# A two-layer hybrid encoder in split fp32: background work tied behind weight splits, loads moved ahead, TensorE's order left to the scheduler

## The chip, the cores and the metric

The kernel runs on one core of a Trainium2 chip. The metric is the device time of one execution in microseconds; the kernel before takes 1553.94 us, the median of three runs (1553.2 to 1554.11).

## What is computed

One sequence of 256 tokens of width 1024 passes two layers. Each layer norms the input, projects it to the inputs of three branches and to their gates, runs the branches, merges them, and ends with a SwiGLU FFN:

```python
h = _rmsnorm(x, norm1_g[l])
(rq, rk, rv, rg, c_q, c_kv, k_rope, s5_u, gate_logits) = jnp.split(h @ w_in[l], split_at, axis=-1)
y_ret = _retention_branch(rq, rk, rv, rg, ...)       # 4 heads, both directions
y_mla = _mla_branch(c_q, c_kv, k_rope, ...)          # latent attention, 8 heads, two inner norms
y_s5 = _s5_branch(s5_u, a_re, a_im, log_dt, ...)     # 64 groups of 64 complex states, both directions, then a GLU
proj = jnp.einsum('bsnk,nkd->bsnd', branches, w_branch[l])
x = x + jnp.sum(sigmoid(gate_logits) * proj, axis=2) @ w_out[l]
h2 = _rmsnorm(x, norm2_g[l])
f_gate, f_up = jnp.split(h2 @ ffn_w_gu[l], 2, axis=-1)
x = x + (silu(f_gate) * f_up) @ ffn_w_down[l]
```

Everything is float32, and the output has the shape of the input.

## The kernel before

**Weights.** All projections multiply a weight tile with activations that lie in SBUF with the tokens along the free axis. A weight tile of 128 x 1024 floats is loaded as `raw` (line 674; five buffers), split into a rounded high part `wh` by ScalarE (line 690) and a remainder `wl` by VectorE (line 691), and used in three matmuls per 128 rows (`mm3`, lines 695 to 697). `half_pair` (lines 735 to 737) does the same for the S5 GLU, half a contraction at a time. A few projections (`fm_pair_native`, line 747) use the raw tile with unsplit float32 matmuls and need no normed input. All loads and stores go through one queue, that of SyncE (SP), by `dma` (line 114).

**Two strands of work.** The trunk (`layer`) emits the projections, the retention heads, the latent attention, the merges and the FFN in program order. S5 is a generator (`s5`) that runs in the background: after each weight tile the trunk calls `tick`, which advances the generator by `step` as long as it has credit; a yield of a number is charged to the credit, a yield of "later" ends the tick. So the program order is the trunk's with S5's instructions woven in.

**S5's parts.** `s5_tables` computes constants from the parameters and sends them through DRAM (`pwd`, `bbd`). `s5_wt` makes one of 16 tables of 128 x 1024 from two loaded constants by two VectorE products and two combinations (lines 547, 548, 551, 552). In layer 0 it does so right before the state matmuls (line 473); layer 1's are made during layer 0's FFN, stored to DRAM (`wtd`) and loaded again in layer 1 (lines 463 and 464). Then come the scan over 32 blocks, and for eight pairs the output tables (`s5_out_tables`, which loads the C matrices through `s`), VectorE products (lines 594 to 596), matmuls (lines 612 and 646), a gather through DRAM (lines 662 and 664) and the GLU.

**Chains that cross engines.** A norm's scale is made in `rstd`: sums by TensorE, a small chain, and a spread matmul (line 834) that is put off to the next weight tile's end by `defer` and `flush`. `ret_heads` normalises a head on VectorE and ScalarE and transposes it on TensorE (line 988) in `finish`, one head later. `early_gates` computes some gate tiles ahead of their use, stores them and loads them back; how many stand between the latent norm's chain and its spread matmul is set by `ng0` and `ng1`.

**What sets the order.** Program order is a priority. A scheduler with a model of the chip places the instructions of each engine's queue by priority and by when their inputs are ready in its model. TensorE is the exception: `run` wraps the whole trunk in `manual_schedule` for TensorE, so its instructions stand in program order.

Of the kernel before, what the change touches and what calls it, by code (L numbers as in the profile page):

```python
# [1 line left out]

# [69 lines left out]
class Kern:  # L72
    def __init__(self, ctx, tc, aps, n4=17, n16=2, nraw=5, nw=3, nwl=3, nwy=4, nwt=2, ntm=2, nev=4, nat=3, r0=75, r1=75, r2=20, delay=1, late=0, e0=2, e1=0, force=0, q0=55, q1=60, nat_u=1, gauss=1, unn=1, ya=0, sp=1, yw=40, yy=30, split=2, m0=4, m1=4, fin=1, dfr=1, nu0=3, nu1=1, pin=0, nl=-1, fw=0, fy=1, ng0=0, ng1=2, tt=1, tp=0, nq0=0, nq1=0, sk=1):
        self.sk = sk
        self.nq = nq0, nq1
        self.tt, self.tp = tt, tp > 0
        self.fw, self.fy = fw, fy
        self.pinm, self.nl = pin, nl
        self.pin = pin > 0
        self.later, self.nu = [], (nu0, nu1)  # L80
        self.fin = fin
# [61 lines left out]
    def step(self):  # L143
        try:
            if self.late:
                with self.tc.high_priority(offset=-self.late):
                    c = next(self.bg)
            else:
                c = next(self.bg)
        except StopIteration:  # L150
            self.bg = None
            return
        if c is None:
            self.credit = min(self.credit, 0.0)
            return
        if c == "later":
            return c
        self.credit -= c
# [124 lines left out]
    def s5_tables(self, l):  # L283
# [72 lines left out]
        return dict(ld={}, PWD=PWD, BBD=BBD, BB2D=BB2D, PXD=PXD, A8=A8, A8s=A8s)  # L356

    def s5_out_tables(self, l, tb, qh):


        nc, V, A = self.nc, self.nc.vector, self.nc.scalar
        cn = self.s4().rearrange("p (d t r q) -> p d t r q", d=2, t=4, r=2)
        for d in range(2):
            for r, k in enumerate(("s5_c_re", "s5_c_im")):
                self.dma(cn[:, d, :, r, :],
                                  self.a[k][l, d, qh * 32:qh * 32 + 32].rearrange("(t g) c p -> (g c) t p", t=4))
        BB2 = self.s(2 * 528, "t_bb2", 1).rearrange("p (d x) -> p d x", d=2)
# [33 lines left out]
    def s5(self, l, ctx, gel_out):  # L401
# [52 lines left out]

        lq = None
        for j in range(8):
            wts = []
            for qq in (2 * j, 2 * j + 1):
# [3 lines left out]
                else:  # L462
                    wt = self.s(1152, "wy")[:, 0:1024]
                    self.dma(wt, wtd[qq])
# [11 lines left out]
            lq = self.s(1152, "wy")[:, 0:512]  # L476
# [78 lines left out]
    def s5_out(self, l, tb, du_load, gel_out):  # L555
# [3 lines left out]
        for j in range(8):  # L559
            qh = j // 4  # L560
            if j % 4 == 0:
                if job:
# [5 lines left out]
                BB2, C1, C2, AB = yield from self.s5_out_tables(l, tb, qh)  # L568
# [33 lines left out]
            yield "later"  # L602
            if job:
                self.s5_emit(job)
# [72 lines left out]
    def wsplit(self, view):  # L677
# [8 lines left out]
        self.parts(f(wh), f(wl), view)  # L686
        return f(wh), f(wl)

    def parts(self, hi, lo, src):
        self.nc.scalar.copy(hi, src)  # L690
        self.nc.vector.tensor_tensor(lo, src, hi.bitcast(F32), ALU.subtract)  # L691
# [251 lines left out]
    def ret_heads(self, l, h, q, k, vt):  # L943
# [52 lines left out]
        last = None  # L996
        for hd in range(RH):
# [4 lines left out]
            if last:  # L1002
                finish(*last)
# [3 lines left out]
            last = hd, yn, th  # L1007
            if not self.fin:
                finish(*last)
                last = None  # L1010
        return y, lambda: finish(*last) if last else None

    def mla_down(self, l, h, rest):
# [11 lines left out]
        ps = self.fm_pair(w, OFF_CQ + 256, h.get)  # L1025
        A.copy(cq[:, 512:768], ps[:, 0:S])
# [197 lines left out]
    def layer(self, l, x2, acc, xg, last):  # L1224
# [7 lines left out]
        pre = [native(0)] if self.nu[l] else []  # L1232
        self.flush(True)
# [121 lines left out]
        r = self.rstd(acc, [D])  # L1355
# [42 lines left out]
    def run(self):  # L1398

        with self.tc.manual_schedule(engines={mybir.EngineType.PE}):  # L1400
            self.trunk()

    def trunk(self):
# [30 lines left out]
        self.begin(0)  # L1434
        self.step()
# [85 lines left out]
```

## Time and profile before

| | us |
|---|---|
| median of three runs | 1553.94 (1553.2 to 1554.11) |
| the profiled execution's own time | 1557.51 |
| its span, first to last instruction | 1555.7 |
| busy: TensorE, VectorE, ScalarE | 1331.0, 1066.0, 757.7 |
| mean granted clock of TensorE | 0.935 |

The profile is one execution of the program. Busy time is that in which an engine executes; idle time before an instruction is put down to what released it last. A row of the timeline is a run of like instructions, with the idle time before it and its releaser in brackets. A window's row gives busy time and instruction count of each engine in a stretch, and the mean granted clock of TensorE, 1.00 for 2.4 GHz and 0.50 for 1.2 GHz.

### The profile page before, as it was taken

How to read it: one execution, taken by the hardware profiler on the slowest of the kernel's cores; microseconds unless marked ns; L12 is line 12 of the kernel's file. 1: busy time of each engine (PE TensorE's matmuls, PEld its weight loads, DVE VectorE, ACT ScalarE, POOL GpSimd, SP SyncE). 2: the span in 40 equal slices, each digit the busy share in tenths (PEclk: the TensorE clock that was granted, in tenths of full speed). 3: DMA queues.
4: the chain of work that ended last, by engine and by line, in shares of the span. 5: the costliest groups of instructions: out<-in, count | busy, mean ns of one | idle time of the engine just before them, and what ended most of it. 6: DMA issues, size and time to landing. Idle time of an engine off the chain costs nothing. (4 is left out here: it accounts for less than half of the span.)

```text
span 1555.7 us, 27234 instructions
## 1 busy us (share of the span) xinstructions
PE 1331.0 (86%) x10858; PEld 1254.1 (81%) x10858; DVE 1066.0 (69%) x1904; ACT 757.7 (49%) x1223; POOL 4.4 (0%) x33
## 2 busy tenths in 40 slices
PE   4967768679888999889888798878997989999997
PEld 3856667679788999879887776768996989999997
DVE  6866877778494887767656665686857735767754
ACT  2633344775633554334333454678555434544442
POOL 0000000000000000000000000000000000000000
PEclk9978888889999999999999999978999989999999
DMA  6858753547765775988788896427675656656662
GB/s 191 271 213 237 197 148 119 137 121 190 205 193 178 216 232 187 266 228 215 206 234 239 249 280 207 132 85 191 182 210 162 193 165 191 175 170 184 187 174 87
DMA packets 425043, 297.46 MB, mean 191 GB/s; under 512 B 29954, under 2 KB 387540, under 8 KB 424916
## 3 DMA queue, kind: packets, MB, share of 16 engines
q1 hardware_dynamic: 424916, 295.73, 66.3%
q8 instruction: 85, 1.39, 0.4%
q14 instruction: 42, 0.34, 0.1%
HBM read 265.01 MB, written 30.67 MB: 190 GB/s over the span
## 5 line engine op out<-in xcount | busy, mean ns | idle before, releaser
L695 PE MATMUL pw<-s,wh 128*128 128x256 f32 x2440 | 720.9, 295 | 37.3 <-ACT wh L690 29.9
L697 PE MATMUL pw<-s,wl 128*128 128x256 f32 x2440 | 708.5, 290 | 43.2 <-DVE wl L691 43.1
L696 PE MATMUL pw<-s,wh 128*128 128x256 f32 x2440 | 707.1, 290 | 6.4 <-DVE s L770 4.1
L690 ACT CAST wh<-raw 128x1024 fp32r<-128x1024 f32 (+4 forms) x394 | 380.7, 971 | 510.2 <-PE pw L696 310.5
L691 DVE TENSOR_TENSOR wl<-raw,wh 128x1024 fp32r<-128x1024 f32 (+4 forms) x394 | 442.9, 1127 | 222.9 <-ACT wh L690 216.4
L695 PEld LDWEIGHTS pw<-s,wh 128*128 128x128 f32 x2440 | 482.7, 198 | 49.9 <-ACT wh L690 32.2
L697 PEld LDWEIGHTS pw<-s,wl 128*128 128x128 f32 x2440 | 482.1, 198 | 49.0 <-DVE wl L691 48.8
L696 PEld LDWEIGHTS pw<-s,wh 128*128 128x128 f32 x2440 | 482.7, 198 | 10.9 <-DVE s L770 5.3
L547 DVE TENSOR_TENSOR wy<-s,s 128x1024 f32<-128x1024 f32 x32 | 39.1, 1222 | 68.3 <-DMA s<-bbd 55.6
L735 PE MATMUL pw<-s,wh 128*128 128x256 f32 x256 | 75.5, 295 | 6.2 <-ACT s L766 6.0
L736 PE MATMUL pw<-s,wh 128*128 128x256 f32 x256 | 75.0, 293 | 1.8 <-DVE s L767 1.8
L737 PE MATMUL pw<-s,wl 128*128 128x256 f32 x256 | 74.7, 292 | 0.8 <-DVE wl L691 0.8
L735 PEld LDWEIGHTS pw<-s,wh 128*128 128x128 f32 x256 | 51.2, 200 | 7.4 <-ACT s L766 6.5
L769 ACT ACTIVATE s<-ev 128x512 fp32r<-128x512 f32 x46 | 29.2, 634 | 50.9 <-DVE ev L1367 30.7
L736 PEld LDWEIGHTS pw<-s,wh 128*128 128x128 f32 x256 | 51.3, 201 | 2.3 <-DVE s L767 2.3
L737 PEld LDWEIGHTS pw<-s,wl 128*128 128x128 f32 x256 | 51.2, 200 | 1.0 <-DVE wl L691 1.0
L594 DVE TENSOR_TENSOR wy<-s,s 128x512 f32<-128x512 f32 x64 | 42.9, 687 | 11.9 <-ACT s L393 8.0
L473 PE MATMUL p<-wy,s 128*32 128x256 f32 x256 | 21.2, 438 | 26.2 <-DVE wy L552 15.2
L595 DVE TENSOR_TENSOR tm<-s,s 128x512 f32<-128x512 f32 x64 | 43.1, 685 | 0.2
L596 DVE TENSOR_TENSOR wy<-wy,tm 128x512 f32<-128x512 f32 x64 | 42.9, 685 | 0.0
L747 PE MATMUL pw<-s,raw 128*128 128x256 f32 x128 | 30.2, 395 | 14.5 <-DMA raw<-in_w_in 14.5
L510 ACT COPY s<-s 64x256 f32<-64x256 f32 (+1 forms) x64 | 40.7, 636 | 1.9 <-DVE s L496 1.1
(290 smaller groups left out, 1504.5 us busy)
## 6 DMA issues: line engine op xcount, KB each, us to landing
raw<-in_w_in SPq DMA_DIRECT2D x122, 512.0 KB
raw<-in_ffn_w_gu SPq DMA_DIRECT2D x88, 512.0 KB
raw<-in_w_branch SPq DMA_DIRECT2D x48, 512.0 KB
s<-pwd SPq DMA_DIRECT2D x64, 256.0 KB
s<-bbd SPq DMA_DIRECT2D x64, 256.0 KB
raw<-in_s_w_glu SPq DMA_DIRECT2D x32, 512.0 KB
raw<-in_ffn_w_down SPq DMA_DIRECT2D x32, 512.0 KB
wt<-kd SPq DMA_DIRECT2D x64, 128.0 KB
```

The source lines that it names most:

```text
L510: A.copy(*todo.pop(0))
L594: V.tensor_tensor(y[:, :, js, :], tv(0), cv(C1), ALU.mult)
L595: V.tensor_tensor(t2, tv(1), cv(C2), ALU.mult)
L596: V.tensor_tensor(y[:, :, js, :], y[:, :, js, :], t2, ALU.add)
L690: self.nc.scalar.copy(hi, src)
L691: self.nc.vector.tensor_tensor(lo, src, hi.bitcast(F32), ALU.subtract)
L695: T.matmul(ps, lh, rh, start=first, stop=False)
L696: T.matmul(ps, lh, rl, start=False, stop=False)
L697: T.matmul(ps, ll, rh, start=False, stop=last)
L735: T.matmul(o, wh[:, k, c], xh, start=(half == 0 and m == 0 and k == 0), stop=(k == 3), **f)
L736: T.matmul(o, wh[:, k, c], xl, start=False, stop=(k == 3), **f)
L737: T.matmul(o, wl[:, k, c], xh, start=False, stop=(k == 3), **f)
```

## The change

1. `run` no longer wraps the trunk in `manual_schedule`: TensorE's order comes from the scheduler, as the other engines' does.
2. The weight split returns its two instructions (ScalarE's and VectorE's), and `step` ties every background instruction it emits behind the last of them, each on its own engine (`issue_after`; an order of issue, no semaphore).
3. `s5_tables` ends with the loads for the first two tables and three yields of "later".
4. The C loads (`s5_load_c`) are taken out of `s5_out_tables` and stand ahead of the gather.
5. Layer 1's stored tables are loaded one pair ahead, and `lq` moves to another buffer.
6. One more "later" in the S5 output after pairs 0 and 4.
7. `ret_heads` keeps two heads' `finish` back instead of one; `mla_down` calls `rest` twice.
8. `ng0` goes from 0 to 3 and `ng1` from 2 to 3 (four more tiles stored and loaded).
9. S5's first step stands after the first native projection instead of before the vectors' loads.
10. Norm 2's spread matmul is put off by one more weight tile.

```diff
-    def __init__(..., ng0=0, ng1=2, ...):
+    def __init__(..., ng0=3, ng1=3, ...):
...
     def step(self):
         try:
-            if self.late:
-                with self.tc.high_priority(offset=-self.late):
-                    c = next(self.bg)
-            else:
+            with ExitStack() as st:
+                for i in self.split_at:
+                    st.enter_context(self.tc.issue_after(i.ins))
                 c = next(self.bg)
...
-        return dict(ld={}, PWD=PWD, BBD=BBD, BB2D=BB2D, PXD=PXD, A8=A8, A8s=A8s)
+        tb = dict(ld={}, PWD=PWD, BBD=BBD, BB2D=BB2D, PXD=PXD, A8=A8, A8s=A8s)
+        for q in range(2):
+            self.s5_fetch(tb, q)
+        for _ in range(3):
+            yield "later"
+        return tb
...
+        ahead = reload(0)
         for j in range(8):
-            wts = []
+            wts, ready = [], ahead
+            ahead = reload(j + 1)
...
-                    wt = self.s(1152, "wy")[:, 0:1024]
-                    self.dma(wt, wtd[qq])
+                    wt = ready.pop(0)
...
             if j % 4 == 0:
+                cn = self.s5_load_c(l, qh)
                 if job:
                     for _ in range(3):
                         yield "later"
                     self.s5_emit(job)
                     yield from self.s5_gather(job, du_load, gel_out)
...
             yield "later"
+            if j % 4 == 0:
+                yield "later"
...
-        self.parts(f(wh), f(wl), view)
+        self.split_at = self.parts(f(wh), f(wl), view)
...
-            if last:
-                finish(*last)
+            if len(last) == 2:
+                finish(*last.pop(0))
...
         ps = self.fm_pair(w, OFF_CQ + 256, h.get)
+        rest()
...
         pre = [native(0)] if self.nu[l] else []
+        if l == 0:
+            self.begin(0)
+            self.step()
         self.flush(True)
...
-        r = self.rstd(acc, [D])
+        r = self.rstd(acc, [D], 1)
...
     def run(self):
-        with self.tc.manual_schedule(engines={mybir.EngineType.PE}):
-            self.trunk()
-    def trunk(self):
...
-        self.begin(0)
-        self.step()
```

How the instructions move at three places follows, as they stand in the queues of the built programs (lines of the changed kernel are some 2 to 22 higher).

SP at the start of the program, ahead of it only the loads of the input and the vectors: `raw` are weight tiles, the `s` tiles are S5's parameters. Before:
```order
L114 DMA sgn<-in_sgn 128x2
L114 DMA s_17_137<-in_s_b_re 32x1x1024 x4
L114 DMA s_18_138<-in_s_b_im 32x1x1024 x4
L114 DMA s_19_147<-in_s_a_re 32x1x64 x4
L114 DMA s_19_147<-in_s_a_im 32x1x64 x4
L114 DMA raw_231<-in_w_in 128x8x128
L114 DMA raw_267<-in_w_in 128x8x128
L114 DMA raw_365<-in_w_in 128x8x128
L114 DMA raw_375<-in_w_in 128x8x128
```
Now:
```order
L116 DMA sgn<-in_sgn 128x2
L116 DMA raw_154<-in_w_in 128x8x128
L116 DMA raw_190<-in_w_in 128x8x128
L116 DMA s_35_203<-in_s_b_re 32x1x1024 x4
L116 DMA s_36_204<-in_s_b_im 32x1x1024 x4
L116 DMA nt_ldt_214<-in_s_log_dt 32x1x1 x4
L116 DMA s_37_213<-in_s_a_re 32x1x64 x4
L116 DMA s_37_213<-in_s_a_im 32x1x64 x4
L116 DMA raw_320<-in_w_in 128x8x128
L116 DMA raw_330<-in_w_in 128x8x128
```
Two weight tiles stand ahead of S5's loads, and the step sizes (`nt_ldt`, which before were earlier in the queue) join those.

VectorE in layer 0's FFN; `wl` is a split's remainder, `wy` a table being made for layer 1, and the last number of a name counts tiles in program order. Before:
```order
L691 TENSOR_TENSOR wl_1191_7011<-raw_1189_7008,wh_1190_7010 128x1024
L547 TENSOR_TENSOR wy_1244_7421<-s4_1206_7142,s4_1205_7139 128x1024
L1366 TENSOR_TENSOR ev_1184_6969<-pw_1176_6907,rs256_1064_6199 128x512
L691 TENSOR_TENSOR wl_1195_7042<-raw_1193_7039,wh_1194_7041 128x1024
L1367 TENSOR_TENSOR ev_1184_6969<-ev_1183_6968,ev_1184_6969 128x512
L548 TENSOR_TENSOR wy_1245_7422<-s4_1206_7142,s4_1205_7139 128x1024
L691 TENSOR_TENSOR wl_1198_7072<-raw_1196_7069,wh_1197_7071 128x1024
L770 SCALAR_TENSOR_TENSOR s16_1066_6201<-ev_1184_6969,s16_1066_6201 128x512
L551 TENSOR_TENSOR wy_1244_7421<-wy_1244_7421,wy_1245_7422 128x8x64
```
Now (lines 566 to 571 are 547 to 552 before, 713 is 691):
```order
L713 TENSOR_TENSOR wl_1173_6846<-raw_1171_6843,wh_1172_6845 128x1024
L1388 SCALAR_TENSOR_TENSOR ev_1168_6833<-ev_1168_6833,ev_1169_6834 128x512
L713 TENSOR_TENSOR wl_1176_6876<-raw_1174_6873,wh_1175_6875 128x1024
L566 TENSOR_TENSOR wy_1179_6909<-s4_1141_6630,s4_1140_6627 128x1024
L1389 TENSOR_TENSOR ev_1169_6834<-pw_1161_6772,rs256_1070_6209 128x512
L567 TENSOR_TENSOR wy_1180_6910<-s4_1141_6630,s4_1140_6627 128x1024
L1390 TENSOR_TENSOR ev_1169_6834<-ev_1168_6833,ev_1169_6834 128x512
L570 TENSOR_TENSOR wy_1179_6909<-wy_1179_6909,wy_1180_6910 128x8x64
L571 TENSOR_TENSOR wy_1179_6909<-wy_1179_6909,wy_1180_6910 128x8x64
L713 TENSOR_TENSOR wl_1185_6921<-raw_1183_6918,wh_1184_6920 128x1024
```
Before, the table tile 7421 stands ahead of splits that the program has some 380 tiles earlier; now a table stands behind the split of number 6876 and ahead of 6921, its place in the program.

TensorE near the end of layer 0's S5, where `p5` are S5's output banks and `pw` with lines 735 to 737 is the GLU. Before:
```order
L696 MATMUL pw_888_4868<-s16_538_2795,wh_893_4901 128x256
L697 MATMUL pw_888_4868<-s16_538_2795,wl_894_4902 128x256
L646 MATMUL p5_895_4929<-wy_860_4660,s4_796_4250 32x128 x4
L646 MATMUL p5_895_4929<-wy_860_4660,s4_797_4252 32x128 x4
L646 MATMUL p5_895_4929<-wt_883_4829,s4_795_4248 32x128 x4
L646 MATMUL p5_895_4929<-wy_863_4671,s4_796_4250 32x128 x4
L646 MATMUL p5_895_4929<-wy_863_4671,s4_797_4252 32x128 x4
L646 MATMUL p5_895_4929<-wt_883_4829,s4_795_4248 32x128 x4
L735 MATMUL pw_897_4959<-s4_774_4148,wh_899_4962 128x256
L736 MATMUL pw_897_4959<-s4_775_4149,wh_899_4962 128x256
```
Now (757 to 759 are 735 to 737 before, 668 is 646, 634 is 612):
```order
L719 MATMUL pw_878_4752<-s16_565_2988,wl_884_4786 128x256
L668 MATMUL p5_885_4813<-wy_855_4598,s4_832_4470 32x128 x3
L668 MATMUL p5_885_4813<-wy_855_4598,s4_833_4472 32x128 x4
L668 MATMUL p5_885_4813<-wt_867_4691,s4_831_4468 32x128 x4
L634 MATMUL p5_886_4839<-wy_871_4707,t_bb2_820_4404 32x128 x8
L757 MATMUL pw_895_4884<-s4_818_4400,wh_897_4887 128x256
L758 MATMUL pw_895_4884<-s4_819_4401,wh_897_4887 128x256
L757 MATMUL pw_900_4920<-s4_818_4400,wh_902_4923 128x256
L758 MATMUL pw_900_4920<-s4_819_4401,wh_902_4923 128x256
L668 MATMUL p5_904_4951<-wy_868_4696,s4_832_4470 32x128 x4
L668 MATMUL p5_904_4951<-wy_868_4696,s4_833_4472 32x128 x4
L634 MATMUL p5_905_4977<-wy_890_4865,t_bb2_820_4404 32x128 x8
```
Before, an S5 block and a GLU half follow each other whole. Now the first matmuls of two GLU halves and two S5 output blocks are interleaved, the blocks ahead of their place.

## Rows read from the trace of the kernel before

**Rows 1.** The page: the span, busy time of each engine, and the granted clock in 40 slices.
```profile
span 1555.7 us, 27234 instructions
...
PE 1331.0 (86%) x10858; PEld 1254.1 (81%) x10858; DVE 1066.0 (69%) x1904; ACT 757.7 (49%) x1223; POOL 4.4 (0%) x33
...
PEclk9978888889999999999999999978999989999999
```

**Rows 2.** The waits of TensorE: us in total, times, longest us.
```profile
PE pw L697 <- DVE wl L691: 43.1, 22, 5.1
PE pw L695 <- ACT wh L690: 29.9, 9, 6.1
PE pa L834 <- ACT ev L827: 15.3, 5, 6.2
PE p L473 <- DVE wy L552: 15.2, 2, 10.3
...
PE pa L988 <- ACT at L981: 14.4, 2, 7.4
PE p L473 <- DMA wy<-wtd: 10.9, 6, 3.6
```

**Rows 3.** Windows: us, busy PE PEld DVE ACT POOL (instructions), granted clock, DMA share, GB/s.
```profile
85.00:107.00 22.00, 6.79 (x39) 4.92 (x38) 13.74 (x16) 1.63 (x2) 0.00 (x0) 0.61 0.55 196
160.00:245.00 85.00, 59.53 (x407) 52.58 (x409) 65.22 (x162) 34.33 (x61) 0.48 (x3) 0.82 0.60 164
345.00:490.00 145.00, 130.97 (x1454) 121.28 (x1454) 102.94 (x147) 75.65 (x141) 1.40 (x10) 0.96 0.70 194
603.00:905.00 302.00, 258.85 (x1957) 250.80 (x1957) 206.74 (x266) 116.91 (x150) 0.00 (x0) 0.94 0.84 235
```

**Rows 4.** Timeline of SP and TensorE, 8 to 38 us: start, us, engine line operation, idle before.
```profile
9.45 2.88 SPq L114 DMA_DIRECT2D s<-in_s_b_re  x4
...
21.01 6.22 SPq L114 DMA_DIRECT2D raw<-in_w_in  x5
...
25.28 5.25 PE L747 MATMUL pw<-s,raw 128*128 128x256 f32 x16 [14.49 <-DMA raw<-in_w_in]
...
37.14 1.03 PE L747 MATMUL pw<-s,raw 128*128 128x256 f32 x4
```

**Rows 5.** Timeline of VectorE and TensorE, 90 to 103 us.
```profile
91.75 1.22 DVE L547 TENSOR_TENSOR wy<-s,s 128x1024 f32<-128x1024 f32 x1 [4.22 <-DMA s<-bbd]
...
95.58 1.08 PE L473 MATMUL p<-wy,s 128*32 128x256 f32 x8 [10.27 <-DVE wy L552]
```

**Rows 6.** Windows of three stretches at half clock.
```profile
89.90:107.00 17.10, 6.48 (x36) 4.82 (x37) 12.08 (x14) 0.59 (x1) 0.00 (x0) 0.50 0.58 213
...
199.10:209.30 10.20, 6.13 (x18) 4.74 (x19) 6.30 (x18) 2.28 (x4) 0.00 (x0) 0.50 0.45 122
...
946.60:950.00 3.40, 3.13 (x21) 1.47 (x17) 0.11 (x1) 0.59 (x1) 0.00 (x0) 0.50 1.11 352
```

**Rows 7.** Timeline of TensorE, the spread matmuls of both layers' latent norms.
```profile
237.79 2.08 PE L834 MATMUL pa<-ev,ones 128*128 128x512 f32 x2 [4.69 <-ACT ev L827]
...
1023.43 2.08 PE L834 MATMUL pa<-ev,ones 128*128 128x512 f32 x2 [6.22 <-ACT ev L827]
```

**Rows 8.** The waits of TensorE and VectorE, 603 to 905 us.
```profile
PE pw L697 <- DVE wl L691: 29.8, 13, 4.7
PE pw L695 <- ACT wh L690: 7.6, 3, 4.8
...
DVE wy L547 <- DMA s<-bbd: 47.6, 11, 8.0
```

**Rows 9.** Timeline of VectorE, 673 to 676 us.
```profile
673.86 1.22 DVE L547 TENSOR_TENSOR wy<-s,s 128x1024 f32<-128x1024 f32 x1 [8.04 <-DMA s<-bbd]
```

**Rows 10.** The page's costliest groups: busy, mean ns, idle before and its releaser.
```profile
L691 DVE TENSOR_TENSOR wl<-raw,wh 128x1024 fp32r<-128x1024 f32 (+4 forms) x394 | 442.9, 1127 | 222.9 <-ACT wh L690 216.4
...
L594 DVE TENSOR_TENSOR wy<-s,s 128x512 f32<-128x512 f32 x64 | 42.9, 687 | 11.9 <-ACT s L393 8.0
```

More of the change, by code (lines that the diff above doesn't have):

```diff
@@ L1 @@
 import math
+from contextlib import ExitStack
 import numpy as np
@@ L72, with __init__ @@
 class Kern:
-    def __init__(self, ctx, tc, aps, n4=17, n16=2, nraw=5, nw=3, nwl=3, nwy=4, nwt=2, ntm=2, nev=4, nat=3, r0=75, r1=75, r2=20, delay=1, late=0, e0=2, e1=0, force=0, q0=55, q1=60, nat_u=1, gauss=1, unn=1, ya=0, sp=1, yw=40, yy=30, split=2, m0=4, m1=4, fin=1, dfr=1, nu0=3, nu1=1, pin=0, nl=-1, fw=0, fy=1, ng0=0, ng1=2, tt=1, tp=0, nq0=0, nq1=0, sk=1):
+    def __init__(self, ctx, tc, aps, n4=17, n16=2, nraw=5, nw=3, nwl=3, nwy=4, nwt=2, ntm=2, nev=4, nat=3, r0=75, r1=75, r2=20, delay=1, late=0, e0=2, e1=0, force=0, q0=55, q1=60, nat_u=1, gauss=1, unn=1, ya=0, sp=1, yw=40, yy=30, split=2, m0=4, m1=4, fin=1, dfr=1, nu0=3, nu1=1, pin=0, nl=-1, fw=0, fy=1, ng0=3, ng1=3, tt=1, tp=0, nq0=0, nq1=0, sk=1):
         self.sk = sk
@@ L80, in __init__ @@
         self.later, self.nu = [], (nu0, nu1)
+        self.split_at = ()
         self.fin = fin
@@ L366, in s5_out_tables @@
                                   self.a[k][l, d, qh * 32:qh * 32 + 32].rearrange("(t g) c p -> (g c) t p", t=4))
+        return cn
+    def s5_out_tables(self, l, tb, qh, cn):
+        nc, V, A = self.nc, self.nc.vector, self.nc.scalar
         BB2 = self.s(2 * 528, "t_bb2", 1).rearrange("p (d x) -> p d x", d=2)
@@ L453, in turn, with reload @@
                 A.copy(o(slice(64, 128), -1), ptv[64:128, r])
+        def reload(j):
+            out = []
+            for qq in (2 * j, 2 * j + 1) if wtd and j < 8 else ():
+                wt = self.s(1152, "wy")[:, 0:1024]
+                self.dma(wt, wtd[qq])
+                out.append(wt)
+            return out
         lq = None
+        ahead = reload(0)
         for j in range(8):
-            wts = []
+            wts, ready = [], ahead
+            ahead = reload(j + 1)
             for qq in (2 * j, 2 * j + 1):
@@ L475, in s5 @@
                              wts[i][:, g4], start=True, stop=True, tile_position=(0, g4 * 32))
-            lq = self.s(1152, "wy")[:, 0:512]
+            lq = self.s(1024, "wt")[:, 0:512]
             A.copy(lq.rearrange("p (q r d x) -> p q d r x", q=2, d=2, r=2),
@@ L567, in s5_out @@
                     job = None
-                BB2, C1, C2, AB = yield from self.s5_out_tables(l, tb, qh)
+                BB2, C1, C2, AB = yield from self.s5_out_tables(l, tb, qh, cn)
                 yq = self.s4().rearrange("p (t q c) -> p t q c", t=8, q=8)
@@ L685, in wsplit @@
             f = lambda t: t.rearrange("p (a b c) -> p a b c", a=shp[0], b=shp[1])
-        self.parts(f(wh), f(wl), view)
+        self.split_at = self.parts(f(wh), f(wl), view)
         return f(wh), f(wl)
     def parts(self, hi, lo, src):
-        self.nc.scalar.copy(hi, src)
-        self.nc.vector.tensor_tensor(lo, src, hi.bitcast(F32), ALU.subtract)
+        return (self.nc.scalar.copy(hi, src),
+                self.nc.vector.tensor_tensor(lo, src, hi.bitcast(F32), ALU.subtract))
     def mm3(self, ps, lh, ll, rh, rl, first, last):
@@ L995, in ret_heads @@
         dec = score(0)
-        last = None
+        last = []
         for hd in range(RH):
@@ L1006, in ret_heads @@
                 dec = score(hd + 1)
[L1007 to L1011, printed above, removed]
+            last.append((hd, yn, th))
+        return y, lambda: finish(*last.pop(0)) if last else None
     def mla_down(self, l, h, rest):
```

3 lines of the change are left out of this document (1 added, 2 removed).

## The prediction, made blind

> **What bounds the kernel now.** I read the summary page first: busy time and clock [rows 1]. TensorE works for 1331.0 of 1555.7 us, VectorE for 1066.0, ScalarE for 757.7. The program is bound by TensorE with holes in it: some 225 us of the span it is not at work, and in the clock line some slices after the start show less than 9 tenths. The list of what TensorE waited for [rows 2] splits the holes: weight splits come late (43.1 us for the VectorE half, line 691, and 29.9 us for the ScalarE half, line 690), the S5 state matmuls of line 473 wait for tables (15.2 us in two waits) and for reloaded tables (10.9 us in six), the retention transposes of line 988 wait 14.4 us, the spread matmul of a norm, line 834, 15.3 us. The windows [rows 3] say how much each stage could give: 85 to 107 us is the S5 states' start, 160 to 245 the end of retention and the latent attention's first norm, 345 to 490 the merges over the end of S5, 603 to 905 layer 0's FFN, where layer 1's S5 tables are built beside it. TensorE is the longest engine in all but the first two; in those VectorE has more to do.
>
> **The change part by part.** The sum stands against the profiled execution, 1557.51 us; the median of the runs is 3.6 us below it, and that is taken off at the end.
>
> *The start.* Before, 16 S5 loads stand ahead of the weights on SP [rows 4]: they are issued from 9.45, the first weight tile at 21.01, and TensorE idles 14.49 us until 25.28. Now two tiles stand in front. The first pair can start 21.01 − 9.45 = 11.6 us earlier, at 13.7. The tiles after it queue behind 20 S5 loads: five groups of four at 2.88 us end near 24.6, and with the 4.3 us that the first tile took from issue to use (25.28 − 21.01) the third one feeds TensorE at 28.9; the row of before has 37.14. That is −8 us; ends 0 (the norm chain holds it) and −11.6. The S5 loads are two issues later, some 1.4 us at 0.72 each; the first S5 table is not needed before 91 us, and has its own term next.
>
> *First state matmuls.* At 95.58 TensorE idles 10.27 us, the longer of the two waits (15.2 us together) [rows 2], for a table that VectorE starts at 91.75 after 4.22 us of waiting for a load [rows 5]. Now the two loads go out when the S5 constants end, and three more weight tiles pass before the table is asked for. Behind the first wait TensorE runs 17.1 us at a granted clock of 0.50, 1.2 GHz, and does 6.48 us of work in it [rows 6]; at full clock half of that, 3.2 us, comes back. Ends 0 and −18.4 (15.2 + 3.2). I take −16: the loads are early enough for all of the waits, but some of the VectorE work remains.
>
> *Retention finish and gate tiles, 160 to 245.* The deferred finish puts a further head of projections between the normalised values and the transposes that waited 14.4 us in two equal waits [rows 2]. Three gate tiles instead of none lie between the norm's chain and its spread matmul, which waited 4.69 us [rows 7]. One of the half-clock stretches of this stage holds 6.13 us of work [rows 6], another 3.1 us back. That makes 22, but VectorE is busy for 65.22 of the 85 us [rows 3], so no more than 19.8 can go. Ends 0 and −19.8; I take −13, two thirds, since VectorE would have to run without a gap for all of it. The eight added transfers are four tiles stored and loaded again, some 5.8 us of SP's time at 0.72; the DMA engines are 0.60 busy in that stage, and nobody waits for SP there. If they cost something it is 5.8 us, inside the ends.
>
> *Layer 0's FFN, 603 to 905.* Idle is 302 − 258.85 = 43.2 us; of it 29.8 are waits for the VectorE split and 7.6 for ScalarE's. VectorE itself stands 47.6 us in front of table products whose constants have not landed [rows 8], once for 8.04 us [rows 9], with the splits behind it. The ties put each table behind the splits traced before it. Ends 0 and −43. I take −24, four fifths of the 29.8, as the loads themselves still come through the same queue; the 7.6 stay. By the Trainium skill, page "DMA: Bandwidth & Descriptors", section "Where 436 GB/s comes from", the memory gives a core some 358 GB/s; at the 235 GB/s of this stage (302 us, 71 MB) that would be 198 us, transfers would bound nothing, and the sum would be up to 19 us lower, near 1463. The row has the DMA engines 0.84 busy at that rate, so the transfers are nearer to a bound than the page has it, and I go by the row.
>
> *Reload one pair ahead (layer 1).* Six waits, 10.9 us, and 3.13 us of work in one half-clock stretch [rows 6], which gives 1.6 back. Ends 0 and −12.5; I take −11, since a tile that is asked for a pair earlier has several weight tiles of time.
>
> *Norms.* The layer 1 norm's spread matmul waited 6.22 us [rows 7] and gets three tiles where it had two; norm 2's is put off by one tile, and has part of the 15.3 − 4.69 − 6.22 = 4.4 us that are left of that wait. Ends 0 and −10.6; I take −7.
>
> *Later S5 output.* Longer holds, the C loads moved up and the extra yield squeeze the four pairs of the second half into fewer places of TensorE's order: 316, counted in the order, instead of 460. VectorE has 48 products there (line 594 is one of three such lines, 64 of each over two layers of eight pairs, so 12 a pair) at 0.687 us, 33 us, and some nine splits at 1.13 us [rows 10], 43 together. TensorE's 316 places are 28 us at the stage's mean of 130.97 / 1454 = 0.09 us. So +15 us; ends 0 (with weight matmuls between) and +25, when the gating products come on top. The C loads come earlier and cost nothing: their wait is short already.
>
> *Splits elsewhere.* Of the 73.0 us of waits for splits, 37.4 are in the FFN; 35.6 are left in S5's and attention's stages. Ends 0 and −36. The ties help where a background product stood in front, but ScalarE and VectorE are as full as TensorE there. I take −8.
>
> *TensorE's order.* Instruction counts are the same on TensorE. Against program order 111 pieces have moved, about two dozen of them S5 blocks 60 to 240 places early. Nothing in the trace prices them; the ends are 0 and 118 us (the second rival). In the main case I take 0, as an early block sits where a split would have been awaited.
>
> Sum: −8 − 16 − 13 − 24 − 11 − 7 + 15 − 8 = −72. 1557.5 − 72 = 1485.5, less 3.6: **1482 us**.
>
> **The rivals.** *First, other waits take the place:* only the start, the first states and the reload pay in full (−35), half of the gate, FFN, norm and split terms pays (−26), and the later S5 output costs its 25. Sum −36: 1518 us. For it: VectorE is at 69% over the span and the DMA engines at 0.84 in the FFN, so a hole that is closed may open one behind it. Against it: TensorE is the longest engine in the two longest of the stages shown.
>
> *Second, slower:* TensorE executes blocks where the order puts them, and a block that stands early holds every weight matmul behind it. If two dozen early blocks each wait for the time of the shorter of the two table waits, 4.93 us (15.2 − 10.27), that is 118 us: −72 + 118 = +46, 1600 us. It decides when the mean stall is over 72 / 24 = 3 us. For it: at 95.58 TensorE was idle 10.27 us with such a block at its head, and the ties now make the block's VectorE work later while its place on TensorE is earlier. Against it: the scheduler knows the ties when it places the blocks. The Trainium skill, page "TensorE: Matmul & The Clock Gate", section "Step-by-step: what each phase is for", says that matmuls stay in program order and only weight loads are pulled ahead; by that rule, with which the 10.27 us wait agrees, no hardware reordering would mend such an order.
>
> *Third, all is covered:* all terms at their lower ends and no new stall: −11.6 − 18.4 − 19.8 − 43 − 12.5 − 10.6 − 36 = −152, 1402 us. For it: TensorE's own work is 1331 us and shrinks further at full clock. Against it: the transfer share in the FFN.
>
> *Fourth, nothing happens:* the moves trade one wait for another of its size, 1554 us.
>
> **How the numbers follow.** The forecast has a chance of 0.50, the first rival 0.20, the second 0.15, the third 0.10, the fourth 0.05. The forecast's own range is 1450 to 1515, from its terms' choices going a third of the way to either end. Eight in ten reaches from 1425, short of the third rival, to 1556, above the fourth, and leaves out the second. A measurement of this kernel tells some 0.2% (3 us) from no change. Faster 0.80, same 0.05, slower 0.15.
>
> **What would show it.** Right: TensorE's first projection starts near 14 us; the waits of line 473's successor shrink from 26 us to under 5; the two 7 us waits ahead of the retention transposes are gone; in the FFN stage VectorE no longer waits for table constants and TensorE's idle time is near 20 us; a wait for VectorE products appears late in S5's output of layer 0. Wrong: S5 blocks at TensorE's head with long idle in front of them (second rival), FFN idle as before at the same DMA share (first rival), or half-clock stretches in new places that eat the gain.

## The result, and the profile after

The changed kernel takes 1515.11 us (median of four runs, 1507.58 to 1520.05); the kernel before, run beside it, 1553.57. The ratio is 0.9747, 95% interval 0.9716 to 0.9777: 38.5 us less (1553.57 − 1515.11), where 72 were forecast. The profiled execution took 1519.22 us, against 1557.51.

The page of the changed kernel, against [rows 1]:
```profile
span 1517.1 us, 27238 instructions
...
PE 1336.3 (88%) x10858; PEld 1245.4 (82%) x10858; DVE 1057.9 (70%) x1904; ACT 755.7 (50%) x1223; POOL 4.3 (0%) x33
...
PEclk9988798989988799999998999979999999999999
```
TensorE does the same number of instructions in about the same busy time; what shrank is its idle time, from 224.7 us (1555.7 − 1331.0) to 180.8 (1517.1 − 1336.3).

The waits of TensorE after (us in total, times, longest us; line 717 is 695 before, 719 is 697, 668 is 646, 492 is 473, 448 transposes S5's input and was 438, and 988 is the retention matmul that was 966, while the transposes of line 988 are now line 1010 and wait 0.6 us):
```profile
PE pw L717 <- ACT wh L712: 35.4, 16, 7.1
PE p L668 <- DMA wt<-kd: 21.2, 21, 5.4
PE pw L719 <- DVE wl L713: 17.9, 25, 1.9
PE p L492 <- DVE wy L571: 11.7, 6, 3.8
...
PE p L448 <- ACT s L442: 9.7, 1, 9.7
...
PE pa L988 <- DVE at L981: 6.3, 2, 6.1
```
Against [rows 2], the wait for VectorE's split fell from 43.1 to 17.9 us and the two 7 us waits of the retention transposes are gone. The wait for ScalarE's split did not shrink (29.9 to 35.4), the wait for `kd`, a reload in S5's output, is now the second longest (21.2 us after 8.1), S5's state matmuls still wait 11.7 us, and the transposes of its input wait 9.7 us, once.

To see where the time went I cut both executions by the count of TensorE's instructions: the first 4000, the next 1500, the next 3500 and the rest. The cuts lie early in layer 0's FFN, at the start of layer 1, and behind layer 1's S5 and GLU, short of its FFN; near them the order of the two kernels differs by little. The windows (columns as in [rows 3]) of the kernel before:
```profile
0.00:616.90 616.90, 495.05 (x4001) 455.85 (x4002) 447.04 (x918) 315.60 (x550) 3.56 (x27) 0.92 0.65 189
616.90:846.90 230.00, 197.98 (x1502) 193.11 (x1501) 158.10 (x212) 82.65 (x104) 0.00 (x0) 0.93 0.86 232
846.90:1321.60 474.70, 415.61 (x3503) 384.18 (x3502) 310.45 (x572) 257.49 (x447) 0.80 (x6) 0.93 0.64 188
```
and of the changed kernel:
```profile
0.00:621.70 621.70, 514.53 (x4000) 461.34 (x4001) 440.94 (x918) 311.91 (x548) 3.49 (x27) 0.90 0.64 190
621.70:831.00 209.30, 189.25 (x1503) 184.61 (x1502) 155.79 (x207) 81.18 (x99) 0.00 (x0) 0.96 0.86 255
831.00:1286.90 455.90, 410.96 (x3503) 378.51 (x3502) 311.00 (x577) 261.02 (x453) 0.80 (x6) 0.94 0.65 197
```
TensorE's counts agree within one, an instruction on the edge of a window. Layer 0 up to its FFN takes 4.8 us longer (621.70 after 616.90), the FFN stage 20.7 less, layer 1 to its FFN 18.8 less, and the rest 3.9 less (1517.1 − 1286.9 against 1555.7 − 1321.6). The forecast had −30 for the first of these stages (start −8, first states −16, retention −13, S5 output +15, splits −8), −24 for the second, −18 for the third: two of three came out, and the first missed by 35 us.

The rows split each stage into busy and idle time of TensorE. In the first stage the idle time fell as well, from 121.85 us to 107.17; what rose is the busy time of the same matmuls, from 495.05 us to 514.53, at a mean granted clock of 0.90 after 0.92. The lower clock would make some 11 us of that (an estimate: 495.05 × 0.92 / 0.90 is 506.05); the rest is open. In the FFN stage 12.0 of the 20.7 us are idle time, and 8.7 are busy time at a clock of 0.96 after 0.93.

### The profile page after: what moved, and what is told of

The parts are those of the page before. It is cut to its first block, busy times and chain, and to the rows that moved or that the text cites. A ratio compares the mean times of both kernels' runs of the same rounds, so it can differ in the third digit from the quotient of the medians.

```text
span 1517.1 us, 27238 instructions
## 1 busy us (share of the span) xinstructions
PE 1336.3 (88%) x10858; PEld 1245.4 (82%) x10858; DVE 1057.9 (70%) x1904; ACT 755.7 (50%) x1223; POOL 4.3 (0%) x33
## 5 line engine op out<-in xcount | busy, mean ns | idle before, releaser
L717 PE MATMUL pw<-s,wh 128*128 128x256 f32 x2440 | 708.9, 291 | 45.0 <-ACT wh L712 35.4
L719 PE MATMUL pw<-s,wl 128*128 128x256 f32 x2440 | 700.8, 288 | 17.9 <-DVE wl L713 17.9
L718 PE MATMUL pw<-s,wh 128*128 128x256 f32 x2440 | 698.2, 287 | 0.2 <-DVE s L789 0.2
L717 PEld LDWEIGHTS pw<-s,wh 128*128 128x128 f32 x2440 | 473.6, 194 | 57.1 <-ACT wh L712 41.4
L719 PEld LDWEIGHTS pw<-s,wl 128*128 128x128 f32 x2440 | 472.5, 194 | 27.4 <-DVE wl L713 25.5
L718 PEld LDWEIGHTS pw<-s,wh 128*128 128x128 f32 x2440 | 474.2, 194 | 3.1 <-issue 1.5
L757 PE MATMUL pw<-s,wh 128*128 128x256 f32 x256 | 74.4, 294 | 5.4 <-ACT s L788 3.5
L759 PE MATMUL pw<-s,wl 128*128 128x256 f32 x256 | 73.8, 290 | 3.5 <-DVE wl L713 3.5
L758 PE MATMUL pw<-s,wh 128*128 128x256 f32 x256 | 73.8, 289 | 0.2 <-DVE s L789 0.2
L757 PEld LDWEIGHTS pw<-s,wh 128*128 128x128 f32 x256 | 50.4, 199 | 7.1 <-ACT s L788 3.9
L759 PEld LDWEIGHTS pw<-s,wl 128*128 128x128 f32 x256 | 50.3, 197 | 4.6 <-DVE wl L713 4.4
L758 PEld LDWEIGHTS pw<-s,wh 128*128 128x128 f32 x256 | 50.4, 197 | 0.5 <-DVE s L789 0.5
L769 PE MATMUL pw<-s,raw 128*128 128x256 f32 x128 | 36.6, 453 | 12.7 <-DVE s L1412 7.6
L668 PE MATMUL p<-wt,s 128*32 128x128 f32 x256 | 28.4, 308 | 21.2 <-DMA wt<-kd 21.2
L769 PEld LDWEIGHTS pw<-s,raw 128*128 128x128 f32 x128 | 29.1, 232 | 18.8 <-DVE s L1412 8.0
```

Of the source, the lines that this page charges most:

```text
L668: T.matmul(po[g4 * 32:g4 * 32 + 32, i * 128:i * 128 + 128], lhsT, rhs, start=(k == 0), stop=(k == 2), tile_position=(0, g4 * 32))
L717: T.matmul(ps, lh, rh, start=first, stop=False)
L718: T.matmul(ps, lh, rl, start=False, stop=False)
L719: T.matmul(ps, ll, rh, start=False, stop=last)
L757: T.matmul(o, wh[:, k, c], xh, start=(half == 0 and m == 0 and k == 0), stop=(k == 3), **f)
L758: T.matmul(o, wh[:, k, c], xl, start=False, stop=(k == 3), **f)
```

## The experiments

The change has three parts that can be had apart: the **ties** (point 2 of the change), the **freed order** of TensorE (point 1) and the **moves** (points 3 to 10). My prediction put everything on ties and moves and nothing on the freed order. The rival theory: the freed order is the gain. Six kernels give all the combinations that were missing.

**Ties and moves, TensorE in program order.** The changed kernel, with

```diff
     def run(self):
+        with self.tc.manual_schedule(engines={mybir.EngineType.PE}):
+            self.trunk()
+    def trunk(self):
```

> The changed kernel with TensorE back in program order (ties and moves only). Theory: the freed order is worth nothing by itself, and the loss of some 28 us near the end of layer 0's S5 comes of the ties and moves: 1510 to 1525 us, with that loss still there. Rival, the freed order holds TensorE at S5 blocks that stand early: 1485 to 1500 us, and the loss goes. Second rival, the freed order is what gains: 1530 to 1555 us.

Measured: 1557.57 us, ratio to before 1.0021 (1.0000 to 1.0043). Above the second rival's range by a little, and far from my theory's: without the freed order the whole of the gain is gone.

**Moves and freed order, no ties.** The changed kernel, with

```diff
-        self.split_at = self.parts(f(wh), f(wl), view)
+        self.parts(f(wh), f(wl), view)
```

> The changed kernel without the ties (moves and freed order). Theory: the ties carry the 26 us won in layer 0's FFN; without them the FFN idles as before, and the S5 output loss of layer 0 shrinks: 1520 to 1540 us. Rival, the ties cost more at the S5 output than they win in the FFN: under 1510 us. Rival, the freed order needs the ties: over 1550 us.

Measured: 1507.2 us, 0.9689 (0.9661 to 0.9717). The ties do not carry the gain: without them the kernel is some 0.6% faster than with them (the intervals just touch).

**Freed order alone.** The kernel before, with

```diff
-        with self.tc.manual_schedule(engines={mybir.EngineType.PE}):
-            self.trunk()
+        self.trunk()
```

> The kernel before with TensorE's order freed and nothing else. Theory (order worth about nothing): 1545 to 1565 us. Rival, order gains: under 1540 us. Rival, S5 blocks stand early and hold TensorE: over 1570 us.

Measured: 1514.07 us, 0.9731 (0.9701 to 0.9762). One line gives as much as the whole change. My theory of an order worth nothing falls here.

**Ties alone.** The kernel before, with the edits to `step`, `wsplit` and `parts` that the change shows, and `split_at = ()` at the start.

> The kernel before with the ties alone, TensorE in program order. Theory: the FFN gains its 24 us and the table waits are not touched, some of it is given back where S5's output is held behind splits: 1525 to 1545 us. Rival, the ties alone do nothing without the early loads: 1550 to 1556 us. Rival, they hold the S5 work on the path: over 1560 us.

Measured: 1542.69 us, 0.9917 (0.9888 to 0.9945): the ties are worth some 0.8%, as my theory had it.

**Moves alone:** the two edits of the first and second experiment together.

> The moves alone: no ties, TensorE in program order. The four runs so far give freed order alone 1514, with the moves 1507, with moves and ties 1515, ties and moves without it 1558, ties alone 1543. If the parts add up, moves alone are 1545 (1552 less the 7 they win beside the freed order). Rival, the moves need the freed order, as their late pieces hold a TensorE in program order: 1555 to 1575 us.

Measured: 1569.48 us, 1.0096 (1.0069 to 1.0123). The moves by themselves are slower. Beside the freed order their median is the better one (0.9689 against 0.9731), but the intervals overlap. The parts do not add up.

**Ties and freed order:** the edits of the third and fourth together.

> Ties and freed order without the moves. If the parts add up: 1514 less the 10 that the ties win alone, 1504 us. Rival, the ties take from the freed order the blocks that it fills holes with, as they do beside the moves (plus 8): 1518 to 1525 us.

Measured: 1506.05 us, 0.9696 (0.9671 to 0.9720). By the medians the ties add 8.0 us to the freed order (1514.07 − 1506.05), near the sum's 10; the intervals of the two ratios overlap.

The stages, cut as above, show which part does what. Each is one profiled execution, in us; executions of one kernel differ by up to some 12 us (the changed kernel's by 1520.05 − 1507.58), so a difference of a few us between two rows says nothing:

| kernel | first 4000 | FFN, 1500 | layer 1, 3500 | rest |
|---|---|---|---|---|
| before | 616.9 | 230.0 | 474.7 | 234.1 |
| ties | 619.3 | 213.2 | 473.3 | 234.3 |
| moves | 640.2 | 223.5 | 471.3 | 232.2 |
| ties, moves | 635.3 | 211.4 | 475.1 | 233.7 |
| freed order | 608.4 | 229.3 | 449.2 | 230.5 |
| ties, freed order | 608.9 | 216.3 | 444.3 | 230.5 |
| moves, freed order | 610.0 | 214.3 | 451.6 | 230.3 |
| all (the change) | 621.7 | 209.3 | 455.9 | 230.2 |

Read it by columns. **The FFN stage** gains by the ties: 16.8 us without any other part, where the freed order alone wins 0.7. It is not theirs alone: moves and freed order without ties have 214.3, which is 15.0 less than the freed order, and the two further kernels of that kind (below) 218.4 and 222.4. **Layer 1** belongs to the freed order: 25.5 us alone, where the ties have 1.4 and the moves 3.4. **The first stage** is where the moves lose: 23.3 us in program order, next to nothing (1.6) beside the freed order, and 12.8 beside freed order and ties, which is no more than executions differ by.

The FFN stage in rows. TensorE's and VectorE's longest waits before, 617 to 847 us:
```profile
PE pw L697 <- DVE wl L691: 23.8, 9, 4.7
```
```profile
DVE wy L547 <- DMA s<-bbd: 38.8, 8, 8.0
```
With the ties alone, 619 to 833 us (line 698 is 697 before, 692 is 691, 748 is 747, 1390 is 1389):
```profile
PE pw L748 <- DVE s L1390: 8.9, 1, 8.9
PE pw L696 <- ACT wh L691: 6.0, 3, 4.8
PE pw L698 <- DVE wl L692: 2.0, 3, 0.8
```
```profile
DVE wl L692 <- ACT wh L691: 47.1, 30, 8.1
DVE ev L1367 <- PE pw L698: 2.4, 4, 0.6
```
VectorE's waits with the freed order alone, 608 to 838 us:
```profile
DVE wy L547 <- DMA s<-bbd: 41.4, 8, 8.2
```
With the ties VectorE's list no longer names table constants (38.8 us before), and TensorE's wait for VectorE's split fell from 23.8 to 2.0 us. With the freed order alone VectorE still stands 41.4 us before them. The changed kernel's rows, 621 to 831 us, agree with the ties':
```profile
PE pw L769 <- DVE s L1412: 7.6, 1, 7.6
PE pw L717 <- ACT wh L712: 7.1, 1, 7.1
PE pw L719 <- DVE wl L713: 2.3, 4, 0.8
```
```profile
DVE wy L566 <- DMA s<-bbd: 3.2, 2, 2.0
```
The first of the ties' rows is a new wait. It stands inside layer 1's first native projection, which needs the last of the FFN's sums; in the ties' run VectorE has that sum queued behind a split for which it stands idle 8.08 us, while ScalarE waits 13.76 us for the weight tile. Each of the five kernels with ties has this wait, of 7.6 to 9.0 us; in those without it is 0.8 at most. So the ties give back a good third of what they win from the splits there.

What moves and freed order win in this stage without ties is another thing. The windows with the freed order alone, and with the moves beside it:
```profile
608.40:837.70 229.30, 199.85 (x1502) 194.97 (x1501) 154.38 (x207) 81.59 (x101) 0.00 (x0) 0.91 0.87 231
```
```profile
610.00:824.30 214.30, 191.33 (x1502) 187.30 (x1501) 154.85 (x207) 81.58 (x100) 0.00 (x0) 0.96 0.83 246
```
More than half of the 15.0 us is busy time (8.5), at a clock of 0.96 after 0.91. VectorE still stands 29.5 us before table constants there, and TensorE 17.3 us before VectorE's splits. Which of the moves does it was not tried.

Why the moves lose in program order: TensorE's waits in that run (line 988 is 966 before, 856 is 834), for the same line 988 beside the freed order, and the window of the first stage in program order:
```profile
PE pa L988 <- DVE at L981: 19.0, 2, 15.0
...
PE pa L856 <- DVE ev L851: 9.2, 1, 9.2
```
```profile
PE pa L988 <- DVE at L981: 8.5, 2, 4.4
```
```profile
0.00:640.20 640.20, 508.36 (x4001) 464.96 (x4002) 441.69 (x916) 312.69 (x548) 3.47 (x27) 0.89 0.62 184
```
In program order one retention matmul waits 15.0 us and a norm's spread 9.2 us, with every weight matmul queued behind; freed, others pass and the two waits of line 988 come to 8.5 us. The waits are a part of the 23.3 us only: TensorE's idle time is 10.0 us more than before (131.84 after 121.85) and its busy time 13.3 us more (508.36 after 495.05), at a clock of 0.89 after 0.92.

**What in the freed order gains.** The order of the built kernel shows two kinds of displaced pieces: S5 blocks ahead of their place or behind it, and trunk pieces that pass each other. Two kernels forbid one kind each, by ties of issue order on the kernel with freed order alone.

S5 never ahead of a trunk instruction that precedes it in the program (`back` holds the instructions traced in `step`; the edges are laid at the end of `run`):

```diff
+    def tie_pe(self, mode):
+        no_sync = mybir.DependencyInfo(mybir.DependencyClass.NoSync, mybir.DependencyReason.DATA)
+        last = {}
+        for i in list(self.traced()):
+            if i.engine != mybir.EngineType.PE:
+                continue
+            me = i.name in self.back
+            prev = last.get(me if mode == "trunk" else not me)
+            if prev is not None and {"early": me, "late": not me, "trunk": not me}[mode]:
+                self.tc.add_manual_dep(i, prev.name, no_sync, reason="pin")
+            last[me] = i
...
         self.trunk()
+        self.tie_pe("early")
```

> The kernel before with TensorE freed, but no S5 instruction of TensorE may stand ahead of a trunk instruction that the program has before it; trunk instructions may still pass S5 ones and each other. If S5 blocks that stand early and fill the waits for weight splits are what gains: 1540 to 1555 us. If what gains is the trunk passing S5 blocks whose inputs are late (as in layer 1's reload), or transposes put off: 1512 to 1525 us.

Measured: 1515.11 us, 0.9752 (0.9722 to 0.9782). S5 blocks that stand early, which my second rival feared and which I then took for the fillers, are worth nothing either way that the intervals show (0.9752 against 0.9731).

The trunk in order among itself: the same with `tie_pe("trunk")`.

> The kernel before with TensorE freed, but the trunk's instructions keep their order among themselves; S5's may stand earlier or later between them. If the play between S5 and trunk is what gains: 1512 to 1525 us. If the trunk's own pieces (retention and attention transposes that are put off, weight matmuls that pass each other) are what gains: 1535 to 1555 us.

Measured: 1546.77 us, 0.9943 (0.9916 to 0.9970). Four fifths of the gain are gone. Its windows (first stage and layer 1), and under them those of the kernel with no early S5:
```profile
0.00:623.10 623.10, 508.25 (x4000) 458.37 (x4001) 448.55 (x921) 314.86 (x550) 3.41 (x27) 0.90 0.65 188
...
850.40:1303.20 452.80, 409.08 (x3502) 377.09 (x3501) 309.63 (x572) 257.78 (x447) 0.79 (x6) 0.95 0.67 197
```
```profile
0.00:602.10 602.10, 502.98 (x4001) 457.25 (x4002) 440.53 (x916) 314.45 (x550) 3.47 (x27) 0.93 0.67 193
...
835.10:1288.10 453.00, 405.05 (x3502) 374.55 (x3501) 308.93 (x574) 257.45 (x449) 0.80 (x6) 0.95 0.68 196
```
Layer 1 keeps its gain in both (452.80 and 453.00 against 474.70 before); of the stages the first differs most, 623.10 against 602.10. (The medians differ by 31.7 us, these two executions by 19.6: the one with the trunk in order was 6 us faster than its kernel's median.) So the two layers gain in different ways. In layer 1 neither early S5 blocks nor a reordered trunk is needed by itself; what both kernels still allow is S5 matmuls that stand behind later trunk instructions. The waits of layer 1 before (847 to 1322 us) and with the order freed (838 to 1287 us) fit that:
```profile
PE pw L697 <- DVE wl L691: 12.3, 8, 5.1
PE p L473 <- DMA wy<-wtd: 10.9, 6, 3.6
```
```profile
PE pw L695 <- ACT wh L690: 15.1, 9, 4.7
...
PE pw L697 <- DVE wl L691: 1.5, 2, 1.1
...
PE p L473 <- DMA wy<-wtd: 0.4, 1, 0.4
```
The state matmuls' wait for reloaded tables, 10.9 us in six, is down to 0.4 us (0.5 with the trunk in order, 1.0 with no early S5), though the loads go out over much the same stretch: from 59.9 to 134.3 us into this window before, from 65.5 to 129.1 with the order freed. Trunk matmuls go first: in the trace 48 of layer 1's 64 state matmuls stand 4 to 25 records of trunk matmuls later than before. The wait for VectorE's split fell too, from 12.3 to 1.5 us, and that for ScalarE's rose from 9.0 to 15.1; together the three give 15 of the 25.5 us. That late S5 blocks are the cause is not shown: each of the two kernels still allows what the other forbids, and one that forbids late S5 blocks was not run. In the first stage the trunk's own pieces have to move: the retention transposes (line 988 in the numbers of before), 14.4 us of waits in [rows 2], are down to
```profile
PE pa L988 <- ACT at L981: 4.6, 4, 2.6
```
with the order freed, since weight matmuls pass them. With the trunk in order they still wait 8.0 us, with no early S5 1.9: a small part of what separates these two kernels.

**Weight matmuls in order, small pieces free.** The same ties among the matmuls of `mm3`, `half_pair` and `fm_pair_native` only:

```diff
-        T.matmul(ps, lh, rh, start=first, stop=False)
-        T.matmul(ps, lh, rl, start=False, stop=False)
-        T.matmul(ps, ll, rh, start=False, stop=last)
+        for i in (T.matmul(ps, lh, rh, start=first, stop=False),
+                  T.matmul(ps, lh, rl, start=False, stop=False),
+                  T.matmul(ps, ll, rh, start=False, stop=last)):
+            self.back.add(i.ins.name)
...
```

> The kernel before with TensorE freed, but its weight matmuls (split triples, GLU halves and the unsplit ones) keep their order among themselves; the small pieces (retention and attention transposes, scores, norm sums and spreads, S5) may move between them. Freed order alone was 1514, trunk in order 1547. If the small pieces that are put off until their inputs are there are what gains: 1512 to 1522 us. If weight matmuls that pass each other are what gains: 1535 to 1550 us.

Measured: 1521.51 us, 0.9759 (0.9702 to 0.9817), at the upper end of the range of the small pieces. Putting off the trunk's small pieces (transposes, scores, norm sums and spreads) gives most of the gain, as S5 pieces free to move without them gave 0.9943; what weight matmuls add by passing each other is not clear of the spread.

**What among the moves loses.** Two kernels take one suspect each out of moves and freed order (1507.2). Without the added yields:

```diff
-        for _ in range(3):
-            yield "later"
         return tb
...
             yield "later"
-            if j % 4 == 0:
-                yield "later"
```

> Moves and freed order without ties (1507), less the added yields of later: the three behind the S5 constants and the one after pairs 0 and 4. Those moves lose some 27 us where layer 0's S5 output ends, in every run that had them. If the yields delay S5 and so cause it: the loss falls under 10 us, 1485 to 1500 us. If the loss is of the gate tiles that no longer cover S5's end: unchanged, 1503 to 1512 us.

Measured: 1511.66 us, 0.9711 (0.9666 to 0.9757): no gain. With the early gate tiles back:

```diff
-ng0=3, ng1=3
+ng0=0, ng1=2
```

> Moves and freed order without ties (1507), with the numbers of early gate tiles back to 0 and 2. If the three gate tiles taken ahead in layer 0 leave S5's end uncovered: the loss there falls under 10 us and the norm's wait of some 5 us comes back, 1485 to 1500 us. If the yields or the other moves are the cause: 1503 to 1515 us.

Measured: 1511.50 us, 0.9708 (0.9655 to 0.9761): no gain either. Neither run can tell the cause, as the base was badly chosen: beside the freed order and without ties, the moves lose next to nothing in the whole first stage (610.0 against 608.4), so there was no loss to take away. The loss at S5's end of which the expectations speak was read from a count of instructions inside the stage, where the runs have a different mix of short S5 and long weight matmuls; over the whole stage this base does not have it.

One wait they do settle. TensorE's wait for the reload `kd` in the base, and without the added yields (line 664 is 668):
```profile
PE p L668 <- DMA wt<-kd: 20.2, 21, 4.5
```
```profile
PE p L664 <- DMA wt<-kd: 9.4, 17, 1.2
```
The other kernels with all the moves have 19.5 to 21.8 us of it, so it comes of the yields. Taking it away makes the kernel no faster.

**The best of it: ties, freed order and one move.** The sixth experiment's kernel, with S5 begun behind the first native projection (point 9):

```diff
-        self.begin(0)
-        self.step()
         self.vectors("vec2", [...])
...
         pre = [native(0)] if self.nu[l] else []
+        if l == 0:
+            self.begin(0)
+            self.step()
         self.flush(True)
```

> Ties and freed order (1506) with one of the moves: S5 begins behind the first native projection, so that two weight tiles are loaded ahead of its parameters. Every run with that move stood some 7 to 8 us ahead by the 500th TensorE instruction. If the stages add: 1498 us, faster than all runs so far. If the S5 strand, started later, takes it back at layer 0's end as in the runs with all moves: 1504 to 1512 us.

Measured: 1480.24 us (median of six, 1475.96 to 1486.90), 0.9512 (0.9474 to 0.9549): the fastest of all, 4.9% under the kernel before. Its page:
```profile
span 1478.5 us, 27232 instructions
...
PE 1324.3 (90%) x10858; PEld 1235.6 (84%) x10858; DVE 1058.8 (72%) x1904; ACT 753.4 (51%) x1221; POOL 4.4 (0%) x33
```
Its stages are 590.3, 213.4, 444.3 and 230.5 us: layer 1 and the rest as with ties and freed order, the FFN 2.9 us shorter, and the first stage 18.6 shorter, where 8 were expected. The start itself gives 7.5 of them (by the 250th TensorE instruction); what the other 11 are was not tried. Against the changed kernel, whose other moves it lacks, the first stage is 31.4 us shorter (621.7 − 590.3; the medians of the two kernels differ by 34.9). So with the ties in place the rest of the moves costs about that much there; which of them is open.

## Why the prediction came near in time and failed in its reasons

The time, 1515 us, lies in the range of eight in ten (1425 to 1556), at the upper edge of the forecast's own (1450 to 1515; its terms' thirds add up to 1455 and 1514), and next to the first rival's 1518; the forecast of 1482 had the sign and twice the gain. That it came so near is luck. The ties and moves, for which the −72 stood, give nothing without the freed order (1.0021), and the gain comes with the term that I put at 0.

- **TensorE's order: the step that failed.** I priced it at 0, with ends of 0 and 118 us of loss, and so left out a gain altogether: I looked at S5 blocks that stand early, and not at matmuls that pass a piece which waits. Alone it measures some −38 us by the medians (1552.14 to 1514.07) and −42 by the ratio (0.9731). The waits that I shared out among the moves were waits at the head of a queue in program order; a freed order alone takes much of them away as other matmuls pass: the reload's from 10.9 us to 0.4, the retention transposes' from 14.4 to 4.6, the norms' spreads' from 15.3 to 7.9. Its rival, S5 blocks standing early and holding TensorE, did not happen: forbidding them changes nothing that the intervals show (0.9752 against 0.9731). The Trainium skill's rule that I set beside this rival ("TensorE: Matmul & The Clock Gate", "Step-by-step: what each phase is for": matmuls keep program order in hardware) cuts the other way here: what the hardware does not reorder, the order built into the queue can. The runs agree: the same ties and moves take 1557.57 us in program order and 1515.11 with the order freed.
- **The start: right.** Forecast −8, with the first pair near 14 us and the third tile at 28.9. The timeline of the changed kernel against [rows 4]:
```profile
11.18 6.61 PE L769 MATMUL pw<-s,raw 128*128 128x256 f32 x16 [0.79 <-DMA raw<-in_w_in]
...
18.44 3.70 PE L769 MATMUL pw<-s,raw 128*128 128x256 f32 x16
...
26.88 11.42 PE L769 MATMUL pw<-s,raw 128*128 128x256 f32 x44 [4.31 <-DMA raw<-in_w_in]
```
The first pair starts at 11.18 and the third tile at 26.88, 10.3 us before the 37.14 of the kernel before; by TensorE's 250th instruction 8.0 us are won (60.1 us after 68.1).
- **First states: wrong.** 15.2 us of waits (two, on line 473) became 11.7 us in six on line 492 and 9.7 on line 448, instead of vanishing. With the moves alone, in program order, 4.7 us are left on line 492; beside the freed order, without ties, 11.0.
- **Retention and gate tiles: right for the wait, wrong for the gain.** The transposes' wait is gone, and either part alone shortens it, the freed order from 14.4 to 4.6 and the moves to 5.6. But with the moves in program order waits of 15.0 and 9.2 us stand elsewhere instead (above).
- **FFN: right, with two terms that I did not have.** Forecast −24 by the ties, measured −20.7 in the changed kernel and −16.8 with the ties alone, through the waits that I named: those for VectorE's split went from 23.8 us to 2.3 and 2.0. The new wait in layer 1's projection takes 7.6 us back, and 8.7 us are busy time at a higher clock. The ties' run moved 251 GB/s in that stage at a DMA share of 0.93, so the 235 before was no ceiling.
- **Reload and norms, layer 1: right number by luck, wrong cause.** Forecast −18, measured −18.8; the moves alone give 3.4, the freed order alone 25.5. In program order the moves do take away the reload's 10.9 us, but other waits take the place, as the first rival has it: in layer 1 the norm's spread waits longer than its 6.22 us before, and the attention's transposes (line 1194), which did not wait there, do (moves alone, 864 to 1335 us):
```profile
PE pa L856 <- ACT ev L849: 9.0, 1, 9.0
PE pa L1194 <- ACT at L1187: 8.8, 2, 6.3
```
- **S5's output: a wait was added, but another one.** TensorE's waits for the reload `kd` in the window 415 to 550 us, after and before:
```profile
PE p L668 <- DMA wt<-kd: 14.4, 13, 5.4
```
```profile
PE p L646 <- DMA wt<-kd: 4.6, 7, 1.1
```
That is 10 us more. But the products on VectorE that I costed hold TensorE for 1.1 us there in all; what is late is the reload, and by the run without the added yields it is those that make it late.
- **Sum.** By stages the whole miss of the sum lies in the first, −30 against +4.8. Its waits did fall (14.7 us less idle time); the busy time, which the sum had only as giving back half-clock time, rose by 19.5 us, at a lower clock. That is one of the prediction's signs of being wrong, half-clock stretches in new places, though by the estimate above the clock explains only about half of it. The moves, costed one by one as gains, are a loss of 23.3 us there in program order.

## What to carry to other kernels

A wait at the head of an in-order queue has two remedies: bring its data earlier, or let other work pass it. Before costing the first, ask whether the change also gives the second, and run it alone; here one line was worth as much as all ten points together (0.9731 and 0.9747), and the other nine without it were worth nothing (1.0021). Gains that were worked out for the same waits do not add up, so test a bundle by its parts: a subset here (ties, freed order and one move) is some 2.3% faster than the bundle by the medians (1480.24 against 1515.11). And read a stage's busy time beside its waits: in the first stage here 14.7 us of waits went and 19.5 us of busy time came.

## What the runs showed of the hardware that I had not expected

Filling TensorE's holes did not raise its clock in step: the changed kernel has 44 us less idle time than before and the same mean granted clock (0.934 after 0.935). The freed order alone, with as much idle time (181.7 us, 1517.4 − 1335.7) and about the same time, has 0.946; its four runs have 0.946 to 0.950, the changed kernel's 0.934 to 0.939. So the sum of the idle time does not settle the clock. In the changed kernel the waits for VectorE's split, for one, are 25 of up to 1.9 us where they were 22 of up to 5.1; whether shorter holes cost as much clock as longer ones was not tried. In the fastest kernel, with 154 us of idle time (1478.5 − 1324.3), it is 0.948.
